# Two decoder layers on one core: another order of the first loads and memsets, other costs and priorities in the list schedule

## The chip, the cores and the metric

The kernel runs on one core of a Trainium2 chip. The core has five engines with a queue each: TensorE (PE) for matrix products and transposes, VectorE (DVE), ScalarE (ACT), GpSimd (POOL) and SyncE (SP), which here issues the transfers between device memory and the core. An engine works its queue off in order; a semaphore makes it wait for another. The metric is the device time of one execution in microseconds. Before the change three runs took 1062.62, 1063.84 and 1065.66 us, median 1063.84.

## The reference

The input x is 512 rows of 1024 numbers. Two layers follow one another, each a mixer and a dense MLP, and each part is `x += RMSNorm_post(f(RMSNorm_pre(x)))`:

```
def even_mixer(h, w_in, lam_re, ..., w_glu, b_f, w_out):      # layer 0
    z = h @ w_in
    u, q, k, v, fl = ...                                       # widths 512, 512, 512, 512, 8
    y_a = s5_mixer(u, ...)                                     # 32 groups of a complex diagonal state space
    y_b = fox_attention(q, k, v, fl, b_f)                      # 8 heads, blocks of 128 queries, forget bias
    return concat([y_a, y_b]) @ w_out

def odd_mixer(h, w_in, pool_w, ..., w_out):                    # layer 1
    z = h @ w_in
    xc, u, v = ...                                             # widths 512 each
    y_c = pool_mixer(xc, pool_w, pool_scale)
    y_d = sgu_mixer(u, v, ln_g, ln_b, w_s, b_s)
    return concat([y_c, y_d]) @ w_out

def sq_relu_mlp(h, w1, w2):                                    # hidden width 4096
    return square(relu(h @ w1)) @ w2
```

## The kernel before, in words

The 512 tokens are four blocks of 128 rows (X0 to X3), the width 1024 is eight blocks of 128. Wide products run in fp32r, a reduced form of float32, with 128 rows of output and up to 512 columns. A float32 operand is split into a rounded part (ScalarE, an ACTIVATE to fp32r) and the rest (VectorE, a TENSOR_TENSOR to fp32r), and a product is three fp32r products (`mm3`). So each weight is loaded by SyncE, rounded by ScalarE, split by VectorE, and then used. Before a mixer or an MLP each token block is normed: ScalarE sums squares into `junk`, GpSimd makes the reciprocal root in two small operations, VectorE scales (a SCALAR_TENSOR_TENSOR of 128x1024 or twice 128x512), TensorE transposes in eight 128x128 pieces into two banks, and ScalarE and VectorE round and split the transposed block. The results of wide products stand in eight banks of PSUM; a bank is free again when VectorE or ScalarE has read it out (an eviction, or, in the MLP, a "collect" that adds it to a 128x512 buffer).

The even mixer is recorded in steps: f (forget gates), z, c, t, o, e (parameters and matrices of the state space, chains of small operations on VectorE), u, q0 to q3 (projections of the heads), a0 to a3 (attention) and s0 to s3 (runs of the state space: a scan on VectorE, whose result goes into 128x128 products). S5D is the code that makes the first state space parameters from lam, log_dt, b and c.

No engine order is written by hand. The code records every instruction as an `Op` (`record`, from L186) with its cost (`cost`, L245), its predecessors and a priority. `issue` (L291) then plays a list schedule: at each moment an engine takes, of the operations whose predecessors are done and whose buffers and banks can be had, the one with the smallest key, and its clock moves on by the cost. The key is made of the place in the recording, of the length of what hangs on the operation (`RANK` is its share) and of a `BOOST` by step; on TensorE, `STICKY` favours a bank that is already begun. `LOOKS` says by phase (0 even mixer, 1 first MLP, 2 odd mixer, 3 second MLP) how far ahead of the oldest waiting user a buffer, a bank or a transfer's buffer may be taken. The list so made is the program: all instructions are emitted by one line (L438, `o.ins = o.fn(*args, **kw)`), which is why nearly all rows of the profile name that line. The transfers recorded ahead of `prog.first` are issued in the order of the recording.

The lines that the first part of the change moves are these, in `tile_trunk`:

```
    SP.dma_start(grow.f(0, DM, slice(0, 2)), mix_pre_g[0].partition_broadcast(2))
    prog.first = len(prog.ops)
    SP.dma_start(lam.f(0, 128, slice(0, 16)), lam_re[0].rearrange("(r g) p -> r (g p)", g=2))
    ...
    load_w()
    load_x0(1)
    for _ in range(3):
        load_w()
    load_x0(2)
    load_x0(3)
```

## Time and profile before

| what | value |
|---|---|
| runs | 1062.62, 1063.84, 1065.66 us |
| profiled execution | 1063.45 us, span from first to last instruction 1061.7 us |
| TensorE busy | 1039.3 us (98%), 5133 instructions |
| VectorE, ScalarE, GpSimd busy | 792.9, 568.5, 57.2 us |
| mean granted TensorE clock | 0.993 |
| read from device memory | 101.55 MB, 98 GB/s over the span |
| longest row of TensorE | 128x512 products, 3842 of them, 904.0 us busy |

A row of a group or a timeline gives the line, the engine, the operation, what it writes and reads (`bank` is a PSUM bank, `b` a buffer, `ct` constants, `small` a column of numbers), the shapes and the count. In a timeline the first number is the start in us, the second the length of the run of like instructions, and the bracket at the end says how long the engine was idle before and what released it. Products overlap a little, so the length of a run reaches beyond the start of the next.

### The profile page before, as it was taken

The numbers are of one execution on the slowest core, as the hardware profiler recorded it, in microseconds if no ns is written. First come the engines' busy times: TensorE is split into PE (matmuls) and PEld (weight loads), VectorE is DVE, ScalarE is ACT, GpSimd is POOL, SyncE is SP. The second block draws the span as 40 slices with busy tenths as digits, with TensorE's granted clock in tenths as the row PEclk, the third lists the DMA queues.
The fourth block names the chain that finished last, engine by engine and source line by source line (L and its number), as shares of the span: only waits on it lengthen the run. The fifth ranks groups of instructions, "written<-read, shape, count | busy, mean of one in ns | idle before, by whom it ended". The sixth has DMA issues, their size and how long they took to land.

```text
span 1061.7 us, 13872 instructions
## 1 busy us (share of the span) xinstructions
PE 1039.3 (98%) x5133; PEld 846.6 (80%) x5133; DVE 792.9 (75%) x1365; ACT 568.5 (54%) x1037; POOL 57.2 (5%) x112
## 2 busy tenths in 40 slices
PE   8999899999999999999999799999999999999996
PEld 5789677788988888888888688889888888888885
DVE  6968899759856586677778998566776697686786
ACT  5474978546744563553653644445645544553641
POOL 4001000003000000000001310011000000000001
PEclk9999999999999999999999899999999999999999
DMA  8221012623314322422514533306134225223212
GB/s 254 68 80 40 2 40 81 218 60 119 120 40 131 120 72 66 143 85 78 160 60 132 156 100 113 106 4 198 39 99 121 98 80 164 75 80 120 79 59 80
DMA packets 110385, 104.53 MB, mean 98 GB/s; under 512 B 9736, under 2 KB 92844, under 8 KB 110318
## 3 DMA queue, kind: packets, MB, share of 16 engines
q1 hardware_dynamic: 110318, 103.66, 31.8%
q8 instruction: 40, 0.66, 0.3%
q14 instruction: 27, 0.22, 0.1%
HBM read 101.55 MB, written 2.10 MB: 98 GB/s over the span
## 4 chain that ended last, share of the span: by engine, by line
PE 89%; ACT 5%; DVE 2%; SPq 1%; issue 1%; POOL 1%; DMA 0%; DVEq 0%; POOLq 0%; ACTq 0%
PE bank L438 89%; ACT b L438 5%; DVE b L438 2%; SPq L438 1%; POOL small L438 1%; DMA b<-in_x_dram 0%; ACT junk L438 0%; DVE small L438 0%; POOL b L438 0%; DVEq L1974 0%; POOLq L1974 0%; ACTq L438 0%; ACTq L1974 0%; DVEq L438 0%; POOLq L438 0%
## 5 line engine op out<-in xcount | busy, mean ns | idle before, releaser
L438 PE MATMUL bank<-b,b 128*128 128x512 f32 (+5 forms) x4684 | 1000.2, 376 | 8.9 <-DVE b L438 8.0
L438 PEld LDWEIGHTS bank<-b,b 128*128 128x128 f32 (+2 forms) x4684 | 810.3, 188 | 182.3 <-DVE b L438 7.2
L438 DVE TENSOR_TENSOR b<-b,b 128x1024 fp32r<-128x1024 f32 (+7 forms) x654 | 483.2, 775 | 128.8 <-ACT b L438 65.2
L438 ACT ACTIVATE b<-b 128x1024 fp32r<-128x1024 f32 (+6 forms) x582 | 376.1, 690 | 261.3 <-DVE b L438 121.9
L438 ACT ACTIVATE b<-bank 128x512 f32<-128x512 f32 (+7 forms) x269 | 131.3, 516 | 148.4 <-PE bank L438 138.2
L438 DVE TENSOR_TENSOR b<-bank,b 128x512 f32<-128x512 f32 (+2 forms) x210 | 120.7, 604 | 50.9 <-PE bank L438 30.9
L438 DVE TENSOR_TENSOR b<-b 128x256 f32<-128x256 f32 (+5 forms) x202 | 91.0, 466 | 36.0 <-PE bank L438 23.9
L438 POOL TENSOR_SCALAR small<-small 128x1 f32<-128x1 f32 x36 | 15.9, 443 | 852.9 <-ACT junk L438 836.7
L438 ACT ACTIVATE junk<-b 128x512 bf16<-128x512 f32 (+1 forms) x32 | 27.0, 843 | 43.5 <-DVE b L438 37.0
L438 PE MATMUL bank<-ct,b 128*128 128x128 f32 (+3 forms) x387 | 43.0, 260 | 5.0 <-DVE b L438 4.5
L438 DVE SCALAR_TENSOR_TENSOR b<-b,small,b 128x1024 f32<-128x1024 f32 (+1 forms) x32 | 36.4, 1150 | 14.8 <-POOL small L438 14.8
L438 PEld LDWEIGHTS bank<-ct,b 128*128 128x128 f32 (+3 forms) x387 | 33.9, 140 | 15.9 <-DVE b L438 6.1
L438 DVE SCALAR_TENSOR_TENSOR b<-b,b 128x512 f32<-128x512 f32 (+2 forms) x28 | 19.0, 686 | 13.9 <-ACT b L438 13.5
L438 POOL TENSOR_TENSOR small<-small,mhalf 128x1 f32<-128x1 f32 x36 | 26.7, 741 | 2.9
L438 ACT ACTIVATE b<-bank,small 128x128 f32<-128x128 f32 (+4 forms) x36 | 19.2, 545 | 7.4 <-DVE small L438 4.5
L438 ACT ACTIVATE junk<-bank 128x512 bf16<-128x512 f32 x16 | 9.5, 594 | 23.3 <-PE bank L438 23.0
L438 DVE TENSOR_REDUCE small<-bank 128x1 f32<-128x128 f32 (+3 forms) x32 | 14.0, 484 | 2.2 <-PE bank L438 2.0
L438 DVE SCALAR_TENSOR_TENSOR b<-b,bank 128x512 f32<-128x512 f32 x16 | 10.9, 681 | 4.8 <-ACT b L438 4.7
L438 POOL MEMSET b<- 128x4 f32 (+4 forms) x27 | 9.2, 375 | 78.7 <-ACT b L438 26.5
L438 DVE TENSOR_SCALAR b<-b,small 128x128 f32<-128x128 f32 (+3 forms) x28 | 9.9, 376 | 1.3 <-POOL small L438 1.1
L438 DVE TENSOR_TENSOR_SCAN b<-b,b 128x512 f32<-128x512 f32 x8 | 9.8, 1221 | 0.2
L438 POOL CAST b<-b 32x512 fp32r<-32x512 f32 (+1 forms) x8 | 5.3, 663 | 65.3 <-ACT b L438 64.9
(41 smaller groups left out, 97.8 us busy)
## 6 DMA issues: line engine op xcount, KB each, us to landing
b<-in_mlp_w_dram SPq DMA_DIRECT2D x128, 512.0 KB, 4.4
b<-in_w_in_even_dram SPq DMA_DIRECT2D x16, 512.0 KB, 6.7
b<-in_w_in_odd_dram SPq DMA_DIRECT2D x12, 512.0 KB, 4.2
b<-in_w_out_even_dram SPq DMA_DIRECT2D x8, 512.0 KB, 3.5
b<-in_w_out_odd_dram SPq DMA_DIRECT2D x8, 512.0 KB, 3.5
b<-in_x_dram SPq DMA_DIRECT2D x7, 512.0 KB, 5.3
out_dram<-b SPq DMA_DIRECT2D x8, 256.0 KB, 2.0
b<-in_s_w_glu_dram SPq DMA_DIRECT2D x2, 512.0 KB, 3.7
```

Of the source, the lines that this page charges most:

```text
L438: o.ins = o.fn(*args, **kw)
```

## The change

The arithmetic and the instructions are the same; what changes is their order, by three means.

1. *First loads and memsets.* The loads of lam and log_dt are recorded behind those of the first four weights and X1, and `prog.first` behind X3, so the forced order of transfers now reaches X3. The loads of b, c and d are recorded just before the first products. `prog.hold` makes every GpSimd operation recorded later wait, in the plan, for the last GpSimd operation of the first norms, so eleven memsets come behind the norms' small operations.
2. *Costs in the plan.* An issue of a transfer costs SyncE 440 ns instead of 60. A transfer takes its bytes by 270 or by 0.36 of the row's bytes, whichever is less. Narrow products (float32 output of at most 64 partitions) cost 13 ns more than their columns instead of 3; a change between narrow and wide adds 125 ns to the clock and `MODE` (8) to the key; a product after a transpose costs 60 ns less.
3. *Priorities.* `LOOKS`, `RANK`, `STICKY` and the table `BOOST` have new numbers.

```
-LOOKS = {0: (202, 21, 10), 1: (186, 29, 7), 2: (48, 11, 15), 3: (36, 8, 6)}
+LOOKS = {0: (114, 26, 16), 1: (302, 58, 20), 2: (11, 12, 6), 3: (85, 18, 11)}
...
-RANK = 0.55
+RANK = 0.5000000000000001
...
-STICKY = 7
+STICKY = 2
+MODE = 8
...
-    "q1": -20, "q3": -5, "q0": 120, "u": -5, "S5D": -20, "s0": 40, "t": 5, "z": -25, "q2": -25, "a0": 85, "a1": 10,
+    "q1": -45, "q3": -15, "q0": 110, "u": -5, "S5D": 10, "s0": 15, "t": 15, "z": -10, "q2": -35, "a0": 50, "a1": 10,
...
@@ record
+            op.narrow = name == "matmul" and ins[0].dtype == F32 and outs[0].shape[0] <= 64
+            op.turn = name == "transpose"
...
+        if self.hold is not None and self.hold.eng == eng:
+            op.preds[id(self.hold)] = self.hold
@@ cost
-            if ins[0].t.dt == BF16 or out.shape[0] <= 64:
-                return max(53, cols / 2.4 + 3)
+            if ins[0].t.dt == BF16:
+                return max(40, cols / 2.4 + 3)
+            if out.shape[0] <= 64:
+                return max(53, cols / 2.4 + 13)
...
-            return v.shape[0] * free(v) * 4 / 270.0
+            src = ins[0].ap if ins and not isinstance(ins[0], View) else args[1].ap
+            row = src[-1][1] * 4 if src[-1][0] == 1 else 4
+            return v.shape[0] * free(v) * 4 / min(270.0, 0.36 * row)
@@ issue
+                            if e == "PE" and o.narrow != narrow:
+                                key += MODE * 1e3
...
-                        clock[e] = now + 60
+                        clock[e] = now + 440
...
+                        if o.narrow != narrow:
+                            ns, narrow = ns + 125, o.narrow
+                        elif turn and not o.turn:
+                            ns -= 60
+                        turn = o.turn
@@ tile_trunk
-    prog.first = len(prog.ops)
-    SP.dma_start(lam.f(0, 128, slice(0, 16)), lam_re[0].rearrange("(r g) p -> r (g p)", g=2))
...
     load_w()
     load_x0(1)
     for _ in range(3):
         load_w()
+    SP.dma_start(lam.f(0, 128, slice(0, 16)), lam_re[0].rearrange("(r g) p -> r (g p)", g=2))
...
     load_x0(2)
     load_x0(3)
+    prog.first = len(prog.ops)
...
-    bt = alloc(512)
-    for o, src in ((0, b_re), (256, b_im)):
...
     wv = [getw() for _ in range(4)]
+    bt = alloc(512)
+    for o, src in ((0, b_re), (256, b_im)):
...
     for w in wv:
         w.free()
+    prog.hold = [o for o in prog.ops if o.eng == "POOL"][-1]
```

How the new list stands beside the old is shown at three places. A row is an instruction with what it writes, what it reads and its shape; the number behind `b_` or `bank_` tells buffers of one list apart and means nothing across the two lists.

The first is the start of SyncE's queue, the order in which the first transfers are issued. Before:

```order
L438 DMA b_74<-in_mix_pre_g_dram 2x1024
L438 DMA b_84<-in_s_lam_re_dram 16x128
L438 DMA b_84<-in_s_lam_im_dram 16x128
L438 DMA b_87<-in_s_log_dt_dram 2x16x1
L438 DMA b_89<-in_w_in_even_dram 128x2x512
L438 DMA b_91<-in_x_dram 128x1024
L438 DMA b_94<-in_w_in_even_dram 128x2x512
L438 DMA b_98<-in_w_in_even_dram 128x2x512
L438 DMA b_100<-in_w_in_even_dram 128x2x512
L438 DMA ct<-cst_dram 128x576
L438 DMA b_103<-in_s_b_re_dram 128x16x16
L438 DMA b_103<-in_s_b_im_dram 128x16x16
```
Now:

```order
L456 DMA b_69<-in_mix_pre_g_dram 2x1024
L456 DMA b_79<-in_w_in_even_dram 128x2x512
L456 DMA b_82<-in_x_dram 128x1024
L456 DMA b_87<-in_w_in_even_dram 128x2x512
L456 DMA b_90<-in_w_in_even_dram 128x2x512
L456 DMA b_96<-in_w_in_even_dram 128x2x512
L456 DMA b_100<-in_s_lam_re_dram 16x128
L456 DMA b_100<-in_s_lam_im_dram 16x128
L456 DMA b_108<-in_s_log_dt_dram 2x16x1
L456 DMA b_111<-in_x_dram 128x1024
L456 DMA b_116<-in_x_dram 128x1024
L456 DMA ct<-cst_dram 128x576
```
The first four weights have moved ahead of lam and log_dt, X1 stands behind the first weight as before, and X2 and X3 (`b_111`, `b_116`) are ahead of the rest of the constants and of b. On GpSimd eleven memsets that stood ahead of and between the first norms' small operations stand behind the eighth of them.

The second is TensorE at the first run of the state space, about 126 us into the execution of before. `bank_1434` and `bank_1437` collect a projection; `bank_1297` and `bank_1319` take the results of the scan (`b_1306` and `b_79` before, `b_1328` and `b_351` now). Before:

```order
L438 MATMUL bank_1434<-b_200,b_976 128x512
L438 MATMUL bank_1434<-b_186,b_990 128x512
L438 MATMUL bank_1434<-b_186,b_976 128x512
L438 MATMUL bank_1434<-b_200,b_976 128x512
L438 MATMUL bank_1297<-b_128,b_1306 128x128
L438 MATMUL bank_1434<-b_186,b_990 128x512
L438 MATMUL bank_1434<-b_192,b_976 128x512
L438 MATMUL bank_1297<-b_134,b_79 128x128
L438 MATMUL bank_1297<-b_113,b_1112 128x128
```
Now:

```order
L456 MATMUL bank_1437<-b_160,b_1000 128x512
L456 MATMUL bank_1437<-b_143,b_1053 128x512
L456 MATMUL bank_1437<-b_149,b_1000 128x512
L456 MATMUL bank_1319<-b_353,b_1328 128x128
L456 MATMUL bank_1437<-b_165,b_1000 128x512
L456 MATMUL bank_1437<-b_149,b_1053 128x512
L456 MATMUL bank_1319<-b_372,b_351 128x128
L456 MATMUL bank_1319<-b_324,b_1180 128x128
L456 MATMUL bank_1319<-b_353,b_1328 128x128
```
The first product with the scan's result stands four wide products earlier in the queue. On VectorE a SCALAR_TENSOR_TENSOR of 64x512 that stood ahead of the group of 128x4x127 multiplications stands behind it.

The third is VectorE where the first MLP passes into layer 1, about 585 us. The SCALAR_TENSOR_TENSOR rows scale and add a token block, those that read `b_5164` before and `b_5136` now make the rows that are transposed, some TENSOR_TENSOR rows of 128x1024 are weight splits (`b_5359` before, `b_5353` now), and rows with a bank and 128x512 free a bank. Before:

```order
L438 TENSOR_TENSOR b_5321<-bank_5278,b_5294 128x2x128
L438 TENSOR_TENSOR b_3206<-bank_5020,b_3206 128x512
L438 TENSOR_TENSOR b_5334<-b_3206,b_5162 128x1024
L438 SCALAR_TENSOR_TENSOR b_5340<-b_2261,small,b_5164 128x1024
L438 SCALAR_TENSOR_TENSOR b_2268<-b_5334,small,b_2268 128x1024
L438 TENSOR_TENSOR b_5359<-b_5303,b_5345 128x1024
L438 TENSOR_TENSOR b_5301<-bank_5348,b_5281 128x2x128
L438 TENSOR_TENSOR b_5308<-bank_5348,b_5287 128x2x128
L438 TENSOR_TENSOR b_3299<-bank_5002,b_3299 128x512
L438 TENSOR_TENSOR b_5311<-bank_5353,b_5290 128x2x128
L438 TENSOR_TENSOR b_5321<-bank_5353,b_5294 128x2x128
L438 SCALAR_TENSOR_TENSOR b_5381<-b_2268,small,b_5164 128x1024
```
Now:

```order
L456 TENSOR_TENSOR b_5321<-bank_5287,b_5304 128x2x128
L456 TENSOR_TENSOR b_5325<-bank_5294,b_5309 128x2x128
L456 TENSOR_TENSOR b_5328<-bank_5294,b_5312 128x2x128
L456 TENSOR_TENSOR b_3277<-bank_4838,b_3277 128x512
L456 TENSOR_TENSOR b_5336<-b_3277,b_5132 128x1024
L456 TENSOR_TENSOR b_3292<-bank_4949,b_3292 128x512
L456 SCALAR_TENSOR_TENSOR b_2180<-b_5336,small,b_2180 128x1024
L456 TENSOR_TENSOR b_5353<-b_5299,b_5341 128x1024
L456 TENSOR_TENSOR b_3292<-bank_4949,b_3292 128x512
L456 SCALAR_TENSOR_TENSOR b_5371<-b_2180,small,b_5136 128x1024
L456 TENSOR_TENSOR b_5382<-b_3292,b_5132 128x1024
L456 SCALAR_TENSOR_TENSOR b_2210<-b_5307,small,b_2210 128x1024
```
Before, the bank `bank_5002` is read out (`b_3299`) behind the scaling `b_5340`, the split `b_5359` and two rows of the transposed block; now the bank `bank_4949` (`b_3292`) is read out ahead of the scaling `b_5371`, and of the weight splits only the fourth (`b_5353`) stands there: the first three are 14, 9 and 8 rows ahead of the first row shown.

22 lines of the change are left out of this document (12 added, 10 removed), and 8 rows, old and new, of the table BOOST.

## The prediction

> **What bounds the kernel now.** I read the page first, then the waits, then the span in stretches, and last the timelines of the stretches that are not full.
>
> ```profile
> PE 1039.3 (98%) x5133; PEld 846.6 (80%) x5133; DVE 792.9 (75%) x1365; ACT 568.5 (54%) x1037; POOL 57.2 (5%) x112
> ...
> PE bank L438 <- DVE b L438: 12.5, 9, 3.4
> ```
>
> TensorE is busy 1039.3 of 1061.7 us, so all that an order can win from waiting is 22.4 us, and 12.5 us of it, in nine waits, is for VectorE. The stretches show where (columns: window, length, then PE, PEld, DVE, ACT, POOL busy, PE clock, DMA share, GB/s):
>
> ```profile
> 0.00:25.00 25.00, 21.89 (x85) 13.28 (x86) 15.75 (x57) 13.62 (x31) 10.31 (x24) 1.00 0.88 249
> 25.00:50.00 25.00, 25.00 (x118) 19.06 (x118) 24.73 (x102) 13.13 (x24) 0.58 (x2) 1.00 0.30 92
> ...
> 125.00:150.00 25.00, 21.20 (x129) 15.45 (x129) 23.14 (x48) 22.99 (x48) 0.31 (x3) 0.93 0.00 1
> ...
> 175.00:200.00 25.00, 24.75 (x171) 18.58 (x170) 24.69 (x50) 17.96 (x39) 0.10 (x1) 1.00 0.25 83
> ...
> 225.00:575.00 350.00, 350.00 (x1629) 288.98 (x1628) 253.66 (x370) 182.19 (x311) 10.34 (x18) 1.00 0.32 99
> 575.00:600.00 25.00, 19.39 (x88) 15.67 (x87) 21.97 (x31) 15.76 (x29) 5.93 (x13) 0.86 0.53 148
> 600.00:1037.00 437.00, 437.00 (x2021) 361.52 (x2020) 320.95 (x475) 219.51 (x370) 18.22 (x28) 1.00 0.31 96
> ```
>
> Two stretches of 350 and 437 us, the two MLPs and most of layer 1, have no idle time: an order wins nothing there. The losses are the start (3.1 us), 125 to 150 (3.8 us and a clock of 0.93) and 575 to 600 (5.6 us and 0.86). In 25 to 50 and 175 to 200 VectorE is as full as TensorE.
>
> **The change part by part.** Each engine holds the same instructions before and after; nothing is removed, added or resized. The sum is therefore made of waits that move, and is made against the profiled execution, 1063.45 us, which is 0.4 below the median of the three runs, 1063.84.
>
> *The start.* The rows of before, from SyncE's queue, GpSimd, VectorE, ScalarE and TensorE:
>
> ```profile
> 3.62 0.40 SPq L438 DMA_DIRECT2D b<-in_w_in_even_dram  x1
> 8.01 6.52 SPq L438 DMA_DIRECT2D b<-in_s_b_im_dram  x1
> 16.33 0.98 SPq L438 DMA_DIRECT2D b<-in_x_dram  x2
> ...
> 1.11 5.59 POOL L438 MEMSET b<- 128x1024 f32 x10
> 6.81 0.30 POOL L438 TENSOR_SCALAR small<-small 128x1 f32<-128x1 f32 x1
> ...
> 9.45 1.41 DVE L438 SCALAR_TENSOR_TENSOR b<-b,small,bank 128x512 f32<-128x512 f32 x2
> ...
> 8.73 1.06 ACT L438 ACTIVATE b<-b 128x1024 fp32r<-128x1024 f32 x1 [3.25 <-DMA b<-in_w_in_even_dram]
> 21.58 0.63 ACT L438 ACTIVATE junk<-b 128x512 bf16<-128x512 f32 x1 [4.05 <-DMA b<-in_x_dram]
> ...
> 11.73 2.36 PE L438 MATMUL bank<-b,b 128*128 128x512 f32 x7 [0.17 <-ACT b L438]
> 24.89 0.63 PE L438 MATMUL bank<-ct,b 128*128 128x128 f32 x4 [0.48 <-DVE b L438]
> ```
>
> Ten memsets fill GpSimd until 6.7 us and hold the first norm's arithmetic (6.81). Behind the norms they hold it no longer; with one more memset gone from inside it, the first scaled rows (9.45) come about 2.1 us earlier. The first weight is issued ahead of three small loads, 1.1 us earlier, and lands by the same 5.1 us (3.62 to 8.73) near 7.6. The first product could start near 9.6 instead of 11.73. But the next weights share the DMA engines (busy 0.88 of this stretch), and ScalarE takes the second row block's squares ahead of the second weight's rounding: walking these rows on in the new order, TensorE waits 3 us in three pieces (1.6, 0.6 and 0.8) before 15.5. Token blocks 2 and 3 no longer stand behind the 6.52 us issue of b_im, so that ScalarE's 4.05 us wait for them ends some 6 us earlier; TensorE felt 0.48 us of it at 24.89, little more. All told −1.3 to +2 us; I take 0. The moved memsets fall where GpSimd has nothing else (0.58 busy in 25 to 50).
>
> *40 to 80 us.* By adding up VectorE's rows in the new order, its S5 parameter chain ends near 35 instead of 41 us, and the splits of the q0 and u weights and the forget-gate chain have 6 to 19 us more of VectorE work ahead of them.
>
> ```profile
> 59.40 1.16 PE L438 MATMUL bank<-b,b 128*128 128x512 f32 x3 [1.18 <-DVE b L438]
> ...
> 62.84 0.69 DVE L438 TENSOR_TENSOR b<-bank,b 128x512 fp32r<-128x512 f32 x1 [3.58 <-ACT b L438]
> ```
>
> VectorE has 0.27 us to spare in 25 to 50, so the later splits come just when TensorE needs them (my walk: one at 42 to 44 for 43.4, one at 53.6 to 57 for about 53.5). The 3.58 us gap at 62.84 covers the rest, and if that cover is gone, attention's first scores wait. The bounds are 0 and +4 (two waits like the 1.18 and the 2.67 us below); I take +1.5.
>
> *The first S5 run, 126 to 134 us.*
>
> ```profile
> 114.55 2.35 DVE L438 TENSOR_TENSOR b<-b,b 128x256 f32<-128x256 f32 x6 [1.11 <-ACT b L438]
> 118.34 1.89 DVE L438 TENSOR_TENSOR b<-b,b 128x256 f32<-128x256 f32 x5 [1.44 <-ACT b L438]
> ...
> 126.50 0.69 DVE L438 SCALAR_TENSOR_TENSOR b<-bank,b 64x512 fp32r<-64x512 f32 x1
> 127.19 4.21 DVE L438 TENSOR_TENSOR b<-b,b 128x508 f32<-128x508 f32 x6
> ...
> 129.82 4.38 PE L438 MATMUL bank<-b,b 128*128 128x128 f32 x23 [2.67 <-DVE b L438]
> ```
>
> TensorE waits 2.67 us for the 508-wide multiplications. In the new order the 0.69 us operation stands behind them, and the two chains whose pauses (1.11 and 1.44) precede them are interleaved, so they can come up to 3.2 us earlier. TensorE asks 0.9 us earlier (four products fewer ahead), which leaves a wait near 0.5. After the wait the clock is down: 0.07 of 25 us is at most 1.75; the 23 products at 129.82 show about 1.2 of it. Gain up to 3.4; nothing, if the later chains of 40 to 80 arrive late here too. I take 2.5.
>
> The 2.67 us wait is shorter than the limit in the Trainium skill, "TensorE: Matmul & The Clock Gate", section "HAM oscillation — how this bites in real kernels", whose rule is that only idle gaps over about 3.4 us throttle TensorE. Here the row of 125 to 150 shows 0.93 after 2.67, so the measurement decides; by the page this term would be 2.2 at most (the wait alone), 1.6 with the same discount, and the time about 1059.
>
> *575 to 605 us, into layer 1.*
>
> ```profile
> 585.59 1.22 DVE L438 TENSOR_TENSOR b<-b,b 128x1024 f32<-128x1024 f32 x1
> 586.73 1.28 DVE L438 SCALAR_TENSOR_TENSOR b<-b,small,b 128x1024 f32<-128x1024 f32 x1
> 588.77 1.28 DVE L438 SCALAR_TENSOR_TENSOR b<-b,small,b 128x1024 f32<-128x1024 f32 x1 [0.76 <-POOL small L438]
> 589.98 1.22 DVE L438 TENSOR_TENSOR b<-b,b 128x1024 fp32r<-128x1024 f32 x1
> 591.11 2.01 DVE L438 TENSOR_TENSOR b<-bank,b 128x256 fp32r<-128x256 f32 x5
> ...
> 588.07 1.09 PE L438 MATMUL bank<-ct,b 128*128 128x128 f32 x8 [2.25 <-DVE b L438]
> 592.51 2.50 PE L438 MATMUL bank<-b,b 128*128 128x512 f32 x5 [3.36 <-DVE b L438]
> 594.81 1.91 PE L438 MATMUL bank<-ct,b 128*128 128x128 f32 x8
> ...
> 567.56 12.75 SPq L438 DMA_DIRECT2D b<-in_w_in_odd_dram  x3
> ```
>
> TensorE waits 2.25 us for the second token block's scaled rows, then 3.36 us for a bank: its eviction (inside 591.11) stands behind a scaling and a weight split. The five products from 592.51 then take 0.46 us each, twice their rate; with the transposes that is 1.9 us more. In all 7.5 us. In the new order the eviction stands ahead of that scaling, three weight splits are done before, and the second block's transposes come behind ten products of the first block. Adding these VectorE rows up from the last common eviction, I find waits of 0.7 to 1.5 for the first block, 1.7 for the bank and 0.3 later: about 3.5 stay, under 3 in one piece. Gain 4; at best 7.5, at worst 0 or below, if the first split waits for its load (second rival).
>
> *Fewer changes between narrow and wide products*: 34 instead of 48, counted in the two orders.
>
> ```profile
> 37.72 13.24 PE L438 MATMUL bank<-b,b 128*128 128x512 f32 x57
> ...
> 103.72 2.46 PE L438 MATMUL bank<-b,b 128*128 128x512 f32 x10
> 106.11 1.93 PE L438 MATMUL bank<-b,ct 64*64 64x512 f32 x8
> ```
>
> 57 wide products take 13.24, or 0.232 each; ten would end at 106.04, and the narrow ones start at 106.11. One change costs some 0.07, fourteen 1.0 us; between 0 and 1.4.
>
> *Elsewhere.* The rest has no idle time to win, but new pauses can appear, most likely in 175 to 200 where VectorE has 0.31 us left: +0.5.
>
> **Sum:** 0 + 1.5 − 2.5 − 4 − 1.0 + 0.5 = −5.5; 1063.45 − 5.5 is 1058.
>
> **The rivals.** *VectorE sets the pace where the waits were.* For it: 23.14 of 25 in 125 to 150, 24.69 in 175 to 200, 21.97 in 575 to 600. What TensorE is spared at 127 and 588 it would wait for some us later. Against: VectorE pauses ahead of both waits (1.11 and 1.44; 0.76 inside the second), and in the first MLP stretch it has 96 of 350 us to spare, so it can enter the second place with no arrears. Half of 6.5 returned with the other terms: 1061 to 1063, no change.
>
> *A VectorE queue held up by a load, slower.* In the new order the split of the first layer-1 weight stands ahead of the evictions of the second MLP output that ran before 572.6. Its load was issued at 567.56 and the loads of this tensor land in a median 4.2 us; with 1.06 for ScalarE and 1.22 for the split this ends at 574, some 2 us behind. In the waits above that is included as far as VectorE pauses. If the buffer comes free 4 us later, the queue, the first block's norm and TensorE shift by as much, the waits grow to 8 and the clock falls (1.9): the term is +5 instead of −4, and the time 1067. It decides from an issue after about 571. Against: the new order brings the load out behind one small load, not six.
>
> *Late weights at 40 to 80.* Both splits miss by 2.7, each with 1.2 to 1.9 of slow clock: about +8 instead of +1.5, 1064.5; with the gain at 127 lost too, 1067. For it: 24.73 of 25. Against: the same work is in the queue, and TensorE has other products to take only if its order holds them ahead, which it does for u.
>
> *All of it lands.* The start wins 1.3, both stalls go (3.4 and 7.5), no new one: 1063.45 − 13.2, or 1050.
>
> **How the numbers follow.** A measurement of this kernel tells about 0.3%, 3.2 us, from no change. The forecast, with its own range of 1054 to 1060.5, has 0.50; all lands 0.10: faster 0.60. VectorE's pace 0.14 and the milder late weights 0.09: within 0.3% 0.23. The held-up queue 0.12 and the harder late weights 0.05: slower 0.17. The range reaches to the rivals on both sides, 1051 to 1066.
>
> **What would show it.** In the new profile: the first product near 9.6 and waits between 11 and 15.5; the 125 to 150 window over 23 us busy at clock 1.00; 575 to 600 over 21 us and at least 0.93; the MLP stretches still full. The forecast is wrong if a wait over 2 us stands between 40 and 65, or if VectorE's first layer-1 weight split waits on its load.

## The result and the profile after

The changed kernel takes 1075.35 us (median of four runs, 1074.09 to 1079.53). The kernel before took 1063.52 beside it, so the ratio is 1.0115 with a 95% interval of 1.0082 to 1.0148. It is slower by 1.15%; 0.5% faster had been forecast, and the time lies outside the range. The profiled execution took 1074.29 us, with a span of 1072.5 and a mean clock of 0.989 (before: 1063.45, 1061.7, 0.993). One execution of a later variant took 2080 us and is left out of its median.

The page and the waits of the changed kernel:

```profile
PE 1045.3 (97%) x5133; PEld 850.2 (79%) x5133; DVE 794.6 (74%) x1365; ACT 571.1 (53%) x1037; POOL 54.9 (5%) x112
...
PE bank L456 <- DVE b L456: 13.8, 16, 3.0
```

TensorE is idle 27.2 us (before 22.4), and it is also 6.0 us longer busy with the same 5133 instructions. So waits are under half of the loss; the rest is work that ran slower. The stretches, with the columns as in the prediction:

```profile
0.00:25.00 25.00, 21.43 (x86) 13.70 (x86) 15.33 (x38) 14.71 (x35) 7.26 (x21) 0.93 0.88 251
25.00:50.00 25.00, 24.60 (x112) 19.86 (x111) 24.62 (x121) 9.61 (x17) 3.40 (x5) 1.00 0.28 90
...
125.00:150.00 25.00, 20.71 (x111) 16.60 (x110) 21.28 (x45) 18.20 (x41) 0.21 (x2) 0.86 0.13 43
150.00:175.00 25.00, 20.68 (x122) 16.32 (x122) 21.58 (x43) 14.13 (x30) 0.21 (x2) 0.80 0.20 64
175.00:200.00 25.00, 24.07 (x172) 19.04 (x170) 21.86 (x37) 16.90 (x33) 0.21 (x2) 1.00 0.13 43
...
225.00:575.00 350.00, 349.86 (x1624) 287.99 (x1624) 251.03 (x365) 185.78 (x316) 10.00 (x16) 1.00 0.31 97
575.00:600.00 25.00, 23.50 (x104) 18.13 (x102) 22.27 (x30) 10.56 (x17) 2.81 (x6) 1.00 0.39 128
600.00:1037.00 437.00, 435.87 (x2007) 357.42 (x2008) 319.59 (x474) 227.04 (x382) 20.34 (x38) 1.00 0.33 101
```

One stretch of the kernel before belongs beside these, and it is one that the prediction did not show:

```profile
150.00:175.00 25.00, 24.80 (x163) 18.96 (x160) 22.73 (x46) 18.18 (x38) 0.21 (x2) 1.00 0.32 105
```

From 575 to 600 TensorE now does 23.50 us of work in place of 19.39, at full clock: the gain that was predicted there. But 150 to 175, nearly full before, is down to 20.68 at a clock of 0.80. In the two long stretches TensorE is as busy as before (349.86 of 350), yet it gets through 1624 instructions instead of 1629, and through 2007 instead of 2021: busy, and slower.

To put the loss in its places, the two traces were laid beside each other by the work done: each TensorE instruction counts a nominal duration for its shape, and the table says how many us later (+) or earlier (−) the same share of that work is reached, gained or lost within each stretch. Stretches are in the time of the kernel before; the row is worked out from the starts of all TensorE instructions. Where the two orders differ, a border such as the one at 154 us can move some microseconds between its neighbours, by the durations that are counted: with the median distance between starts for each shape, 4.5 us of the changed kernel's loss fall just before 154 and 4.4 behind. The sums over 118 to 184 us (+8.8) and 118 to 211 us (+10.0) do not depend on it.

| stretch, us | 0–35 | 35–118 | 118–154 | 154–184 | 184–211 | 211–558 | 558–613 | 613–1048 |
|---|---|---|---|---|---|---|---|---|
| changed kernel | +1.6 | −0.2 | −0.3 | **+9.1** | +1.2 | +0.8 | **−4.4** | **+3.1** |

The largest term by far stands in a stretch where the kernel before had nothing to wait for. These are TensorE's rows there, then VectorE's (timeline of the changed kernel: start, length of a run of instructions, the shape of its first one, and in brackets the idle time before and what ended it):

```profile
154.77 1.50 PE L456 MATMUL bank<-b,b 128*128 128x512 f32 x17
159.27 6.49 PE L456 MATMUL bank<-b,b 128*128 128x128 f32 x32 [3.00 <-DVE b L456]
165.69 0.66 PE L456 MATMUL bank<-ct,b 128*128 128x128 f32 x4
166.28 0.65 PE L456 MATMUL bank<-b,b 64*64 64x128 f32 x6
167.57 0.33 PE L456 MATMUL bank<-ct,b 128*128 128x128 f32 x1 [0.65 <-ACT b L456]
168.58 5.07 PE L456 MATMUL bank<-b,b 128*128 128x512 f32 x14 [0.68 <-ACT b L456]
...
156.07 3.65 DVE L456 TENSOR_TENSOR b<-b,b 128x508 f32<-128x508 f32 x6
159.64 2.14 DVE L456 TENSOR_REDUCE small<-bank 128x1 f32<-128x128 f32 x5
```

At 156 the second S5 run reaches its six 508-wide multiplications on VectorE, and TensorE stands 3.00 us for them. Behind them in VectorE's queue are the maxima of an attention block's softmax, so ScalarE's exponentials, the transposes and the next S5 products come late as well. The kernel before has the same six instructions there (five of them from 152.95 us on), but it has wide products to do beside them. The lines of 152 to 173 us, grouped by shape, for before and then for the changed kernel:

```profile
L438 PE MATMUL bank<-b,b 128*128 128x512 f32 x44 | 12.2, 406 | 0.0
```

```profile
L456 PE MATMUL bank<-b,b 128*128 128x512 f32 x15 | 5.8, 532 | 0.7 <-ACT b L456 0.7
```

In the new order 15 wide products stand where 44 stood. The mean of one grows from 406 to 532 ns, and after the wait the clock is down:

```profile
155.00:165.00 10.00, 7.00 (x45) 6.35 (x46) 10.00 (x22) 4.28 (x10) 0.11 (x1) 0.68 0.00 0
165.00:175.00 10.00, 8.67 (x43) 6.54 (x40) 6.64 (x15) 6.04 (x15) 0.00 (x0) 0.80 0.34 107
```

In these 20 us TensorE idles 4.33 us and the clock gives away 0.32 and 0.20 of 10 us, or 5.2; together 9.5, near the 9.1 of the table.

### The profile page after: what moved, and what is told of

It reads as the page before. It is cut to its first block, busy times and chain, and to the rows that moved or that the text cites. A ratio compares the mean times of both kernels' runs of the same rounds, so it can differ in the third digit from the quotient of the medians.

```text
span 1072.5 us, 13870 instructions
## 1 busy us (share of the span) xinstructions
PE 1045.3 (97%) x5133; PEld 850.2 (79%) x5133; DVE 794.6 (74%) x1365; ACT 571.1 (53%) x1037; POOL 54.9 (5%) x112
## 4 chain that ended last, share of the span: by engine, by line
PE 84%; DVE 7%; ACT 4%; DMA 1%; issue 1%; POOL 1%; SPq 0%; DVEq 0%; POOLq 0%; ACTq 0%
PE bank L456 84%; DVE b L456 7%; ACT b L456 3%; ACT junk L456 1%; POOL small L456 1%; DMA b<-in_w_in_odd_dram 1%; DMA b<-in_w_in_even_dram 1%; SPq L456 0%; DVE small L456 0%; DVE mst L456 0%; DVEq L1992 0%; POOLq L1992 0%; ACTq L456 0%; POOL b L456 0%; ACTq L1992 0%
## 5 line engine op out<-in xcount | busy, mean ns | idle before, releaser
L456 PE MATMUL bank<-b,b 128*128 128x512 f32 (+6 forms) x4684 | 1007.4, 379 | 15.0 <-DVE b L456 11.0
L456 PEld LDWEIGHTS bank<-b,b 128*128 128x128 f32 (+3 forms) x4684 | 814.3, 189 | 190.2 <-issue 11.1
L456 DVE TENSOR_TENSOR b<-b,b 128x1024 fp32r<-128x1024 f32 (+8 forms) x654 | 482.7, 774 | 128.2 <-ACT b L456 72.6
L456 ACT ACTIVATE b<-b 128x1024 fp32r<-128x1024 f32 (+6 forms) x582 | 380.7, 692 | 270.0 <-PE bank L456 152.1
L456 ACT ACTIVATE b<-bank 128x512 f32<-128x512 f32 (+6 forms) x269 | 131.6, 516 | 153.2 <-PE bank L456 144.6
L456 DVE TENSOR_TENSOR b<-bank,b 128x512 f32<-128x512 f32 (+3 forms) x210 | 121.2, 603 | 63.4 <-PE bank L456 50.0
L456 DVE TENSOR_TENSOR b<-b 128x512 f32<-128x512 f32 (+5 forms) x202 | 90.3, 459 | 35.4 <-PE bank L456 18.1
L456 POOL TENSOR_SCALAR small<-small 128x1 f32<-128x1 f32 x36 | 18.2, 504 | 838.5 <-ACT junk L456 817.3
L456 POOL TENSOR_TENSOR small<-small,mhalf 128x1 f32<-128x1 f32 x36 | 21.7, 604 | 3.0
L456 DVE SCALAR_TENSOR_TENSOR b<-b,small,bank 128x512 f32<-128x512 f32 x8 | 6.0, 750 | 4.3 <-POOL small L456 4.3
```

## The experiments

Every run of a variant is compared with the kernel before on the same chip, whose medians lay between 1063.4 and 1063.9 us. The stretches of ten of the variants, made as above:

| stretch, us | 0–35 | 35–118 | 118–154 | 154–184 | 184–211 | 211–558 | 558–613 | 613–1048 |
|---|---|---|---|---|---|---|---|---|
| changed, old loads | +3.4 | +0.3 | +0.7 | +0.1 | +2.3 | +1.9 | −3.3 | +3.3 |
| changed, STICKY 7 | +2.6 | +0.4 | +1.9 | +7.6 | +3.4 | +1.0 | −2.8 | +3.8 |
| late numbers only | −0.6 | +0.1 | 0.0 | 0.0 | 0.0 | +1.3 | 0.0 | +5.5 |
| loads and hold only | +4.1 | +1.9 | +6.4 | +10.7 | +4.9 | +2.8 | 0.0 | +2.9 |
| late numbers, RANK 0.5 | +1.1 | +0.5 | +7.2 | +9.1 | +1.6 | +2.1 | −0.5 | +5.9 |
| hold only | +1.5 | −0.3 | +6.3 | +0.3 | +0.9 | +1.4 | +1.0 | +2.7 |
| numbers only | +4.1 | +5.7 | +2.2 | +2.9 | +5.2 | −1.3 | −4.2 | +1.1 |
| numbers of first MLP | −0.5 | 0.0 | +0.1 | +0.1 | +0.2 | −1.0 | −3.7 | +0.7 |
| changed, tiles first | +2.2 | −0.4 | −0.7 | +5.7 | +1.2 | −3.5 | −4.6 | −3.9 |
| before, tiles first | −0.3 | −0.1 | +0.1 | +0.1 | −0.1 | −3.3 | −0.5 | −3.9 |

### Where wide products are missing

**The first loads back in their old order**, the rest of the change kept:

```
+    prog.first = len(prog.ops)
     SP.dma_start(lam.f(0, 128, slice(0, 16)), ...)
...
     load_x0(3)
-    prog.first = len(prog.ops)
```

> The changed kernel with the first loads recorded as before (prog.first early, b, c and d loads ahead of the parameter code); new costs, numbers and the hold stay. In its TensorE order the longest stretch of the even mixer without eight wide projection products holds 5.7 us of other work, against 11.7 in the change and 6.8 before. Theory A (the 9 us lost at 155 to 184 come from attention a1 and state space run s1 standing together without wide products): that loss goes, and the 1.5 us of the start; the slower second MLP (+3) and the gain at 585 (-5) stay: 1062 to 1066. Theory B (the new costs and numbers lose the time in the even mixer whatever the loads): 1070 or more.

Measured: 1070.56 us, ratio 1.0063 (1.0046 to 1.0080). The 9.1 us at 154 to 184 are gone (+0.1), with all new costs and priorities still in place. TensorE is busy 25.00 of 25 us from 150 to 175:

```profile
150.00:175.00 25.00, 25.00 (x180) 19.35 (x180) 23.14 (x48) 19.83 (x42) 0.41 (x3) 1.00 0.18 66
```

So under the new costs and numbers the clump needs the new loads; other parts of the change make losses near it by themselves, as the next runs show. The time falls by only 4.8 us, since the start is worse (+3.4) and 2.3 us go at 184 to 211: by its time the run lies in the range of theory B, and only the stretch speaks for theory A.

**The new loads and the hold alone**, in the kernel before (the second and third parts of the change, costs and numbers, left out):

```
+        if self.hold is not None and self.hold.eng == eng:
+            op.preds[id(self.hold)] = self.hold
...
+    prog.first = len(prog.ops)
     SP.dma_start(ct[:, 256:C_END], cst[:, 256:C_END])
```

> The kernel before with the first loads and the hold of the change alone; costs and numbers as before. Longest stretch without eight wide products 18.1 us of other work (6.8 before, 11.7 in the change). Theory A (the stretch sets the loss): the start loses 1.5 to 2.5 us as in the change and the even mixer 10 us or more, 575 to 605 as before: 1074 to 1080. Theory B (the new numbers and costs lose the time): 1062 to 1067.

Measured: 1095.51 us, ratio 1.0292 (1.0274 to 1.0309). Without the new costs and numbers the loads and the hold do nearly three times the harm of the whole change. Between 118 and 211 us 22 us go. The largest wait:

```profile
150.71 0.45 PE L441 MATMUL bank<-ct,b 128*128 128x128 f32 x1 [4.10 <-DVE b L441]
```

**The stickiness back to 7.** The edit is one number, `STICKY = 7`; it asked whether changes between banks slow the products.

> The changed kernel with STICKY 7 instead of 2. The order of the even mixer is nearly the same (longest stretch without wide products 11.7 us of work, as in the change); from the first MLP on wide products change the bank 802 times in their order instead of 1282 (743 before). Theory A (changing the bank costs about a nanosecond or two per product and makes the second MLP 0.7% slower): 128x512 products in the MLPs back to 229.9 ns from 231 to 231.7, 3 to 4 us less, 1071 to 1072.5. Theory B (the products' rate differs between runs or chips): rate and time as in the change, 1074.5 to 1076.

Measured: 1080.64 us, ratio 1.0168 (1.0151 to 1.0185). The share of long products that go to another bank than the one before fell from 0.46 to 0.28 in the first MLP, and the product stayed at 231.3 ns there: bank changes are not what slows it. The clump is still there (+7.6), and the time is longer than either theory had it.

**Thinning VectorE's work at that place**, in the changed kernel and in the kernel before, each in its own order. Four of the six 508-wide instructions of the second S5 run of layer 0 are done on 16 of their 508 columns; most of that run's carry is left out.

```
+        prog.thin = 4 if cb == 1 and prog.phase == 0 else 0
         mul(a0, e1, m3)
         sub(sr, sr, a0)
```

> The changed kernel in its own order, with four of the six 128x508 VectorE instructions that end the second S5 run of layer 0 (3.65 us at 156.07) done on 16 columns of 508: it leaves out most of the carry of that run. It takes about 2.2 us from VectorE where TensorE has no wide projection products to go on with. Theory (there TensorE runs at the pace of VectorE's queue, and the half clock follows from the wait): the wait of 3.00 us at 159.27 becomes 0.5 to 1.2, no half clock from 159 to 164, the loss between 154 and 184 us against the kernel before falls from 9.3 to between 3 and 6, and the time is 1068.5 to 1072 us. Rival (the stretch is bound by the chain of softmax, transposes and ScalarE, or by the clock alone): the loss stays at 8 or more, 1073.5 to 1076 us.

> The kernel before in its own order, with the same four VectorE instructions on 16 columns (the same part left out). Theory (here the wide products cover the same VectorE work, 44 of them between 152 and 173 us): 0 to -0.8 us, 1062.4 to 1063.8. Rival (this VectorE work is on the path in either order): -1.8 us or more, 1061.7 or less.

Measured: the changed kernel 1072.73 us (1070.36 to 1075.42), the kernel before 1063.74, ratio 1.0002 (0.9993 to 1.0011). The thinning takes 2.0 us from VectorE (the six take 1.64 us in place of 3.65). In the kernel before these are free, as expected. In the changed one the named wait falls from 3.00 to 1.27:

```profile
157.40 2.69 PE L461 MATMUL bank<-b,b 128*128 128x128 f32 x22 [1.27 <-DVE b L461]
160.96 0.87 PE L461 MATMUL bank<-b,b 64*64 64x128 f32 x10 [0.87 <-ACT b L461]
163.66 0.33 PE L461 MATMUL bank<-ct,b 128*128 128x128 f32 x1 [0.67 <-ACT b L461]
164.67 5.08 PE L461 MATMUL bank<-b,b 128*128 128x512 f32 x14 [0.68 <-ACT b L461]
```

The stretch loses 5.3 us instead of 9.1, inside what the theory gave. But three other variants with the changed order and nothing thinned (two of the paddings and the tiles laid first, below) lose 5.7 there too, in executions in which the clock stayed at 1.00 between 155 and 175. The clock has to be kept apart to compare them. The thinned execution did lose clock, behind 165 us:

```profile
155.00:165.00 10.00, 6.51 (x61) 5.27 (x61) 9.84 (x25) 6.80 (x14) 0.11 (x1) 1.00 0.19 63
165.00:175.00 10.00, 10.00 (x50) 7.78 (x49) 5.97 (x15) 7.07 (x17) 0.00 (x0) 0.83 0.12 44
```

TensorE idles 3.49 us in these 20 us, and the clock gives away 1.7 more. In two of the three executions that kept the clock (one padding, and the tiles laid first) it idles 5.21 and 5.22 in the same windows. So the 2.0 us taken from VectorE took about 1.7 us of idle time from TensorE: VectorE's multiplications do set its pace there. They are only the first link, a chain through ScalarE stands right behind (the waits of 0.87, 0.67 and 0.68), and the median falls by 2.6 us where up to 6.9 had been expected. Without wide products TensorE follows whichever chain is there.

**The hold alone, and the numbers alone**, each in the kernel before:

```
+    prog.hold = [o for o in prog.ops if o.eng == "POOL"][-1]
```

```
-LOOKS = {0: (202, 21, 10), 1: (186, 29, 7), 2: (48, 11, 15), 3: (36, 8, 6)}
+LOOKS = {0: (114, 26, 16), 1: (302, 58, 20), 2: (11, 12, 6), 3: (85, 18, 11)}
...
-RANK = 0.55
+RANK = 0.5000000000000001
...
-STICKY = 7
+STICKY = 2
...
```

> The kernel before with the hold of GpSimd's operations alone; loads, costs and numbers old. For the start: theory A (the hold, which the changed kernel, the one with old loads and the one with new loads have in common, makes the start longer): +1 to +3 us at 35 us of the program. Theory B (it is the order of the first loads): within 0.6 us there. For the stretch from 118 to 211 us: the fewest wide products in any 10 us of the planner's TensorE work are 12 in the kernel before, 4 in the changed one, and 3 here; theory (too few wide products beside softmax and S5 run): +9 us or more there, and 1073 us or more; rival (the clump needs more than that): under +5, under 1069.

> The kernel before with the new numbers alone (looks, priorities, share of the rank, stickiness); old loads, no hold, old costs. The fewest wide products in any 10 us of the planner's TensorE work are 17 here. Theory (no stretch without wide products, so no loss): within 0.7 us at 35, between -2 and +3 us from 118 to 211, -4 to -5.5 at 575 to 613, +1 to +3 in the products of the MLPs, in all 1057 to 1063 us. Rival (the numbers carry the loss by some other way): +6 or more from 118 to 211, 1066 us or more.

Measured: the hold alone 1077.07 us, ratio 1.0127 (1.0114 to 1.0141); the numbers alone 1082.49, ratio 1.0178 (1.0163 to 1.0193). The three parts tried alone so far are each worse than the whole (the new costs alone were not tried): none can be given a price of its own, since each changes what the list makes of the others. The hold by itself makes the start 1.5 us longer, as much as in the changed kernel (1.6). It loses 7.5 us between 118 and 211, between the 9 or more of the theory and the under 5 of the rival, at a place without wide products (first row). The numbers alone refute the simple form of the theory. By the plan every 10 us of theirs hold at least 17 wide products, and yet 10 us are lost from 118 to 211 (second row):

```profile
146.98 1.70 PE L441 MATMUL bank<-ct,b 128*128 128x128 f32 x6 [3.07 <-DVE small L441]
```

```profile
142.76 6.02 PE L438 MATMUL bank<-b,b 128*128 128x512 f32 x25 [3.63 <-ACT b L438]
```

In the second row the instruction that waits 3.63 us is itself a wide product. By the program it writes the bank that held the attention scores of 138.33 us, and that bank comes free only when ScalarE has read them. So filler needs a free bank and a place ahead of what waits; a count of wide products in 10 us of the plan does not foretell the loss.

### The gain at 575 to 605 us

**The new numbers of the later phases alone**, in the kernel before (`LOOKS` 1 to 3 and the entries of `BOOST` that the MLPs and layer 1 use), and the same with `RANK = 0.5` and the small tile of the section after this one padded:

```
-LOOKS = {0: (202, 21, 10), 1: (186, 29, 7), 2: (48, 11, 15), 3: (36, 8, 6)}
+LOOKS = {0: (202, 21, 10), 1: (302, 58, 20), 2: (11, 12, 6), 3: (85, 18, 11)}
```

> The kernel before with the new LOOKS and BOOST of phases 1 to 3 alone; even mixer in the order of before, STICKY 7, RANK 0.55, old costs and loads. Theory A (the 5.3 us gained at 575 to 605 belong to the new priorities of the later phases): profile to 225 us as before, waits of at most 3 us in all at 575 to 605, 1057.5 to 1060. Theory B (the gain comes from the new costs of transfers or from how the earlier part arrives): 1062 to 1066.

> The kernel before with RANK 0.5, the new LOOKS and BOOST of phases 1 to 3, and mst padded; costs, loads, STICKY and the even mixer's numbers as before. In its orders the longest stretch without wide products is 6.3 us of work (6.8 before), and on VectorE at the third place the splits stand 12, 9 and 7 rows ahead of the first block's scaling and the bank's eviction 8 rows behind it, as in the run with STICKY 7, which gained 4.2 us there. Theory A (the stretch, the place of the eviction and the addresses set the time): the even mixer as before within 2 us, 575 to 605 gains 4 to 5, products near 229.2: 1056 to 1060. Theory B (the gain at 575 to 605 needs the new costs): 1060 to 1064.

Measured: 1071.65 us, ratio 1.0077 (1.0062 to 1.0092), and 1088.75, ratio 1.0232 (1.0215 to 1.0249). Both missed what was expected. In the first the gain is absent, and one wait takes the place of the two. TensorE stands for a bank whose eviction starts on VectorE at 588.45 us. Between the first block's scaling (580.19) and that eviction VectorE has three weight splits; before, one split stands between the first block's scaling and the eviction that ends the wait of 3.36, and in the changed kernel none:

```profile
589.18 1.65 PE L432 MATMUL bank<-b,b 128*128 128x512 f32 x3 [4.95 <-DVE b L432]
```

In the second, the changed share of the rank reorders the first mixer too, which was meant to stay as it was, and 17.9 us go between 118 and 211, so it says nothing on the gain (−0.5 between 558 and 613).

**The new numbers of the first MLP alone, from that phase on**, with the first mixer's order untouched:

```
+RANKS = [0.55, 0.5, 0.5, 0.5]
+STICKS = [7, 2, 2, 2]
...
-                                key -= STICKY * 1e3
+                                key -= STICKS[o.phase] * 1e3
...
```

> The kernel before, with its own order through the first token mixer; from the first MLP on, the new share of the rank and the new stickiness, and the new looks and priorities of the first MLP alone (those of layer 1 and its MLP stay old). Theory (the gain at 575 to 613 us is the place of one eviction in VectorE's queue at the end of the first MLP, and needs nothing of the rest of the change): no difference up to 560 us beyond 0.5 us, then -4 to -5.5 between 558 and 613, and in all 1057.5 to 1060 us. Rival A (the new order of the MLPs costs time in every product, as in the late numbers alone, 0.9 and 3 us): 1061 to 1064. Rival B (the gain is lost again at 707 to 731, where the late numbers alone lost 2.5 us): 1060.5 to 1062, with a VectorE wait near 730.

Measured: 1059.80 us (1059.23 to 1060.40), ratio 0.9964 (0.9951 to 0.9977): faster than both kernels. The stretch from 558 to 613 gives 3.7 us, no stretch ahead of it differs by more than 1.0, and TensorE is busy 22.76 us of the window at full clock in place of 19.39 at 0.86:

```profile
575.00:600.00 25.00, 22.76 (x111) 17.83 (x111) 21.84 (x28) 13.63 (x26) 8.32 (x15) 1.00 0.38 106
```

### Why full stretches are slower

In the MLPs TensorE has hardly any idle time in any version, but a product of 128x512 takes 230.0 and 229.6 ns from start to start before (first and second MLP), and 230.9 and 231.5 in the changed kernel. With 1536 such products in each MLP that is 1.4 and 2.9 us, near the +0.8 and the +3.1 of the table.

The buffers get their addresses in the order in which the program first uses them, and a small tile (`mst`, 8 columns, 32 bytes) lies between them. So the order decides at which side of it a buffer lies, and with it the low bits of its address. Sorted by whether the streamed operand and the weights loaded beside it have the same address modulo 256, pairs of the kernel before take 228.8 ns where they are alike (1875) and 233.5 where they are not (424). In the changed kernel it is 230.1 (1366) and 232.9 (922): the unlike pairs are twice as many. The alike ones are slower beside unlike ones: in the kernel before, alike pairs whose neighbours are alike too take 228.0 ns (1142), those with an unlike pair among the two before or the one after 230.7 (601).

**The small tile padded**, to 16 columns, together with another padded to 16, and to 32, all in the changed kernel; and to 16 in the kernel before. The order stays as it was:

```
-    mst = fixed(8, F32, "mst")
+    mst = fixed(32, F32, "mst")[:, 0:8]
```

> The changed kernel with the small fixed tile mst made 64 bytes long instead of 32 (16 columns, 8 used): the order of every engine is the change's, word for word, and all of the 51 pooled buffers now start at an address that leaves 32 when divided by 64 (in the change 12 of them start at a multiple of 64; before, 6). Theory A (a 128x512 product is slower when its weights or its columns are read from a multiple of 64; in the traces so far 232.8 ns against 230.4 in the change and 233.2 against 229.1 before): the products go to 229 to 229.5 ns, 3842 times some 2 ns, 1066 to 1070. Theory B (the products are slower because of the order or of the run): rate and time as in the change, 1074.5 to 1076.5.

> As the run before it, with mhalf padded to 64 bytes too, so that all pooled buffers start at a multiple of 64; the order is the change's. Theory A: every product pays, 232 to 233 ns, 1077 to 1081. Theory B: 1074.5 to 1076.5.

> The changed kernel with one small tile of 8 columns padded to 32, so that all the 4096-byte buffers lie alike modulo 128 bytes; the order of the instructions is the changed kernel's. Theory (an address bit that differs between the streamed operand and the weights loaded beside it makes the long products slower, so the 230.9 and 231.5 ns of the two MLPs come from where the buffers lie): 229.4 to 230.2 ns a product in both MLPs, and 1068 to 1072 us. Rival (it comes with the order, or with something else than the low address bits): 230.6 ns or more and 231.2 or more, and 1073 to 1076 us.

> The kernel before with mst padded to 64 bytes; 4 of the 6 buffers that started at a multiple of 64 now leave 32. Order as before. Theory A: products 229.66 to 229.1 ns, 1060 to 1062. Theory B: 1062.5 to 1064.5.

Measured: 1074.70, 1073.55 and 1072.45 us, ratios 1.0108 (1.0091 to 1.0125), 1.0092 (1.0067 to 1.0116) and 1.0092 (1.0070 to 1.0115); the kernel before 1062.62, ratio 0.9990 (0.9980 to 0.9999). The product stays at 230.5 to 230.8 and 231.0 to 231.6 ns. The first thought, an alignment to 64 bytes, falls: with all buffers alike modulo 64 nothing changes. But the unlike pairs only moved to another address bit: with the tile 128 bytes long, pairs that differ in bit 7 take 232.0 ns against 230.1.

**All small tiles laid first**, so that no buffer is shifted against another modulo 2048; done to the changed kernel, to the kernel before and to the one with the first MLP's numbers, and in the last of them once more with all buffers moved together by 160 bytes:

```
+        for v in self.fixed:
+            v.t.get()
         for o in order:
```

> The changed kernel, order untouched, with all small tiles that live through the program laid first in memory, so that every 4096-byte buffer lies alike modulo 2048 bytes. In the changed kernel, and in its copy padded to 128 bytes, a product is slower by 2.7 and 1.9 ns where the streamed operand and the weights loaded beside it lie on different sides of such a tile. Theory (the offset between the two, at whatever address bit, is what costs): 229.0 to 229.9 ns a product in both MLPs in place of 230.9 and 231.5, and 1067 to 1071 us. Rival (which side matters, or the order itself, not the offset): 230.4 or more and 230.9 or more, 1072 to 1076 us.

> The kernel before, order untouched, with all small tiles that live through the program laid first in memory, so that every 4096-byte buffer lies alike modulo 2048 bytes, as in the two runs that came to 1064.43 us (the changed kernel) and 1050.85 us (first MLP's new numbers). Theory (where the buffers lie sets the product's time, whatever the order): 227.0 to 227.5 ns a product in both MLPs in place of 229.98 and 229.56, and 1053.5 to 1056 us, so that the new numbers of the first MLP are again worth 3 to 5 us, and the changed kernel is 9 to 11 us slower in the like layout. Rival (the layout helped the new orders only): 229.3 ns or more, 1061 to 1064 us.

> The kernel before with the first MLP's new numbers (1059.80 us), and all small tiles that live through the program laid first in memory; its order is untouched. Theory of the offset: 229.0 to 229.6 ns a product in both MLPs in place of 229.75 and 230.19, and 1057.0 to 1059.2 us. Rival: rates as they were, within 0.2 ns, and 1059.3 to 1060.5 us.

> The kernel of 1050.85 us with all its buffers moved by 160 bytes together: still alike modulo 2048, but at 160 modulo 256, where most buffers of the kernel before lie, in place of 0; its order is untouched. Theory A (it is enough that streamed operand and weights lie alike): 227.0 to 227.5 ns a product, 1050 to 1052 us. Theory B (they must also begin at a multiple of 256, or of some smaller power of two): 228.4 to 229.2 ns, 1055 to 1059 us.

Measured: changed kernel 1064.43 us (1056.81 to 1069.05), ratio 1.0000 (0.9979 to 1.0020); kernel before 1055.75 (1055.15 to 1056.58), ratio 0.9929 (0.9916 to 0.9941); first MLP's numbers 1050.85 (1050.46 to 1051.42), ratio 0.9881 (0.9868 to 0.9893); the same moved by 160 bytes 1050.98, ratio 0.9884 (0.9869 to 0.9900). The product takes 227.0 to 227.4 ns in all four, in both MLPs. The second MLP's 265 us, busy throughout, hold this many TensorE instructions. Kernel before:

```profile
770.00:1035.00 265.00, 265.00 (x1156) 216.39 (x1155) 191.47 (x279) 134.59 (x217) 0.00 (x0) 1.00 0.32 98
```

Changed kernel:

```profile
770.00:1035.00 265.00, 265.00 (x1147) 214.63 (x1146) 185.22 (x273) 136.65 (x220) 0.00 (x0) 1.00 0.32 98
```

Changed kernel, small tiles first:

```profile
770.00:1035.00 265.00, 265.00 (x1167) 218.15 (x1166) 191.12 (x280) 135.88 (x217) 0.00 (x0) 1.00 0.31 98
```

Kernel before, small tiles first:

```profile
770.00:1035.00 265.00, 264.90 (x1166) 217.58 (x1165) 193.38 (x283) 132.72 (x216) 1.07 (x2) 1.00 0.31 99
```

So the slower products of the change are a matter of where buffers lie, and no property of its order: laid alike, both orders run at the same 227.2. It is the like offset that counts, not the alignment, since 160 bytes for all change nothing. The gain was larger than expected, 229.0 ns or more having been forecast for the product: even the alike pairs of the kernel of 1059.80 us were slower (229.0 ns) than the mean is now.

Laid alike, the changed kernel is 8.7 us behind the kernel before, and the first MLP's numbers are worth 4.9. The kernel with the first MLP's numbers and the tiles laid first is the best of the study: 12.8 us, or 1.2%, ahead of the kernel before.

### The clock as a part of the loss

The twelve runs of the changed kernel with its tiles laid first spread over 12 us. The fastest had a mean clock of 0.999 and the slowest 0.985; 0.014 of 1063 us is 15. So the time lost to the clock is enough for all of the spread, and over the twelve runs time and clock go together. In its profiled execution the clock did not drop in the clump at all (two windows, then the row of the wait):

```profile
155.00:165.00 10.00, 6.13 (x59) 4.90 (x58) 10.00 (x21) 5.22 (x11) 0.11 (x1) 1.00 0.14 51
165.00:175.00 10.00, 8.65 (x51) 6.73 (x50) 7.42 (x18) 8.26 (x20) 0.00 (x0) 1.00 0.18 56
```

```profile
159.08 3.00 PE L459 MATMUL bank<-b,b 128*128 128x128 f32 x22 [2.79 <-DVE b L459]
```

TensorE idles 5.2 us there, at full clock, and the stretch loses 5.7; in the changed kernel it idled 4.3 and lost 5.2 more to the clock. A wait of 2.79 went unpunished here, one of 3.00 halved the clock there, and 2.67 did so at 127 us in the kernel before. The Trainium skill ("TensorE: Matmul & The Clock Gate", section "HAM oscillation — how this bites in real kernels") names idle gaps over about 3.4 us as those that throttle. No gap of the changed kernel is that long (the longest is 3.0), so by these runs shorter gaps throttle too, in some executions.

The traces also tell which executions. Behind its first rise, every stretch between two changes of the clock, in all twenty traces, is a whole multiple of 3.413 us long: the clock changes on a grid of cells of that width, and the grid lies differently in each execution. From 20 us on, each of the 28 full-clock cells in which TensorE was idle for 1.9 us or more is followed by a half-clock cell. Of the 44 with 1.3 to 1.9 us 10 are, and of the 5847 with less 2. The wait of 3.00 us puts 2.40 into one cell (155.3 to 158.7); the one of 2.79 is divided by a border into 1.52 and 1.27. Short waits add up: from 141.6 to 145.0 the changed kernel idles 1.36 us in pieces of at most 0.64, and the next cell is at half clock. What decides between 1.3 and 1.9 us is open. So the part of the loss that the clock makes depends on where a wait falls on the grid. That this is also what sets the twelve runs apart fits, but is not shown, as only one execution of each kernel was traced.

## Why the prediction was wrong

**The step that failed is "Elsewhere", put at +0.5**, "most likely in 175 to 200". It measured about +14: 9.1 at 154 to 184, 1.2 at 184 to 211, and 3.9 in the two MLPs. Two things were wrong in it.

The first is its premise that where the kernel before has no idle time only little can be lost. The trace of before tells where its own order waits, not where another order will. From 150 to 175 VectorE was busy 22.73 of 25 us, and TensorE was full only because 44 wide products stood ahead of what waited. The new order was walked on at the four places where the old one stalled, and not here. That the clump causes the loss is shown in so far as the old loads, which dissolve it, remove all 9.1 us. VectorE's multiplications are its first link: 2.0 us less of them took 1.7 of some 5.2 us of idle time. The rest of the chain was not taken apart, and up to 5.2 us of the 9.1 are half clock, which other executions of the same order did not have.

The second is "the MLP stretches still full" as a sign that nothing happens there. They are full, and slower: 3.9 us by the offsets between buffers. Neither the order nor any row of busy time showed that; the count of instructions in a full window does.

**The start**, taken as 0, is +1.6 at 35 us, inside its bounds. Half of its steps came true: the norms start earlier (GpSimd's first arithmetic at 5.58 in place of 6.81, the first scaled rows at 6.59 in place of 9.45). The first weight did not. It was issued 1.14 us earlier and was rounded 0.84 later, at 9.57, after a wait for its transfer:

```profile
2.48 0.40 SPq L456 DMA_DIRECT2D b<-in_w_in_even_dram  x1
...
9.57 1.06 ACT L456 ACTIVATE b<-b 128x1024 fp32r<-128x1024 f32 x1 [4.08 <-DMA b<-in_w_in_even_dram]
...
10.95 0.50 PE L456 MATMUL bank<-b,b 128*128 128x512 f32 x1 [1.65 <-ACT b L456]
```

"Lands by the same 5.1 us" was wrong: it took 7.1, with the same four transfers issued behind it as before; why, no run tells. By 9 us the queue had finished 1.91 MB, against 1.81 before, so the early issue brought hardly more in. The clock was also down there, from 11.9 to 15.3 us, but a copy of the same order that kept it (the small tile padded to 16) reached the block of 22 products at 18.04 us, this one at 17.94: it was not the clock that set the pace. What of the 1.6 us comes from the weight, and what from the hold, which alone costs 1.5, was not separated further; the variants whose start keeps the order of before differ from it by up to 0.6.

**40 to 80 us**, put at +1.5 for late weight splits: between 35 and 100 us +1.9 were measured, with one wait of 1.42 for VectorE at 55.63. Of it 2.1 come back by 118, so late weights are no lasting part of the loss. **The first S5 run**, put at −2.5, gave nothing: +0.2 between 118 and 135. The run's chain did not come earlier; the wait stands there as before, at 2.79 instead of 2.67, and the rival in which VectorE's pace remains was right for this place. The prediction's own sign failed here: 125 to 150 holds 20.71 us at a clock of 0.86, where over 23 at 1.00 had been named. The wait:

```profile
130.17 5.30 PE L456 MATMUL bank<-b,b 128*128 128x128 f32 x27 [2.79 <-DVE b L456]
```

**575 to 605 us**, put at −4, was right: −4.4 between 558 and 613, −3.7 where the first MLP's numbers alone were changed. The mechanism was the eviction's place in VectorE's queue, as predicted: from 575 on no wait is longer than 1.11 us, the clock stays at 1.00, and the first layer-1 split waits only 0.29 (for its rounding, which waited 1.41 for the load). The variant with three weight splits ahead of the eviction confirmed it from the other side. **Fewer changes between narrow and wide products**, −1.0, can't be told apart: from 60 to 118 us the sum of everything is −1.0, and the late splits that were made good are in it.

The range was too narrow on the slow side because all its rivals lived at the four places. None of them gives the loss: the held-up queue at 575 did not come, and the harder late weights did not either.

## What to carry to other kernels

When a list scheduler moves everything, walk the new order also where the old one was full, above all where a second engine is over nine tenths busy, and look for stretches in which the waiting instruction has no independent work ahead of it in its queue. Compare full stretches by the instructions they hold, not by busy time: a kernel can lose half a per cent with every window full. And before the parts of a schedule are judged by their times, lay the buffers alike, since a new order also deals out new addresses.

## What the runs showed of the hardware

- A 128x512 fp32r product took 227.2 ns where all buffers lie alike modulo 2048, and 229.6 to 231.5 on average where a 32-byte tile shifts some against others; in the kernel before, unlike pairs took 233.5 on average and alike ones 228.8. Shifts of 32, 64 and 128 bytes each showed it; 256 did not (in the kernel before, pairs 256 bytes apart took 228.9, as much as those at the same offset). Moving all buffers by 160 bytes changed nothing. The Trainium skill ("SBUF — State Buffer", section "Operand start alignment") says where an operand may start and adds that this is about legality, not speed; these runs show a price in speed that such a rule does not cover. Part of it falls on alike pairs next to unlike ones (230.7 against 228.0). Why it arises stays open.
- TensorE's clock changed on a grid of 3.413 us that lies differently in each execution. Each of 28 full-clock cells with 1.9 us or more of idle time was followed by a half-clock cell, 10 of 44 with 1.3 to 1.9 and 2 of 5847 with less. So a wait of 2.79 us, divided by a border, cost nothing, and one of 3.00 halved the clock. Twelve runs of one kernel differed by 12 us while their mean clock went from 0.985 to 0.999.
- A weight issued 1.14 us earlier, right behind the first rows of x, was ready 0.84 us later: an earlier issue is no earlier landing.
